# A gated hybrid attention block in float32: the up projection as three matmuls of 256 columns into one half bank, without the copy and addition of two parts

## The chip, the cores and the metric

The kernel runs on one core of a Trainium2 chip. The metric is the device time of one execution in microseconds, as the median of the runs shown. The core's engines work side by side on queues of their own: TensorE multiplies matrices (PE in the profile, and PEld for its loading of weights), VectorE (DVE) and ScalarE (ACT) work on rows of numbers, GpSimd is POOL, and SyncE (SP) issues most transfers from memory.

## The reference, cut to what matters

The block has 256 tokens of width 2048. It mixes three kinds of attention through gates and an output projection, and then runs a feed-forward part of width 5632, all in float32. The change lies in the feed-forward part alone, in the product with `w_up`:

```
h2 = rms_norm(x, g_ffn[l])
u = causal_depthwise_conv(h2 @ w_up[l], conv_w[l], conv_b[l])
u_gate, u_val = jnp.split(u, 2, axis=-1)
x = x + (jax.nn.silu(u_gate) * u_val) @ w_down[l]
```

`h2 @ w_up` is a product of 256 x 2048 by 2048 x 11264. The convolution runs along the tokens, over three of them.

## The kernel before

A float32 product is made here of three products of float32r, the form that TensorE takes at a higher rate. Each operand is split into two parts: `hi`, the value rounded to float32r, and `lo`, the rest. A product is then hi x hi + hi x lo + lo x hi, and lo x lo is dropped. Activations are kept as tiles whose 512 columns are the 256 columns of the hi part followed by the 256 of the lo part (`xT`, `oT`, `mT`, `hT`, `aT`).

Weights come in through `piece`: a transfer on SP's queue brings 128 x 1024 numbers into `raw`, ScalarE rounds them into `hi` (L136), and VectorE subtracts to get `lo` (L137). There are four buffers of each kind. Most stages take the result of `piece` into `passes` (L147 to L149): there the activation is the stationary operand (128 x 128), the weights stream past it with up to 512 columns, and three matmuls in a row add into the same output.

The up projection is turned the other way. There the weights are stationary, 128 of their columns at a time, and the activation `hT` streams past, so that the result has features on partitions and the 256 tokens along its columns, as the convolution wants it. The columns of `w_up` are taken in 22 stripes of 512: for `f0` in steps of 4 over 44 feature tiles, and for `s` = 0 (gate) and 1 (value). A stripe has four feature tiles, each with a bank of PSUM (128 x 512 float32) of its own, from a pool of eight banks. Over 16 tiles `k + j` of the contraction, and for each of the four, two matmuls are issued (L739 and L740): the first takes the `hi` weights past all 512 columns of `hT`, so that hi x hi lands in the left half of the bank and hi x lo in the right half; the second takes the `lo` weights past the left 256 columns of `hT` and adds lo x hi to the left half. That is 44 x 2 x 16 = 1408 pairs.

`conv` then ends a feature tile. ScalarE copies the right half out of PSUM into `cr` (L710), VectorE adds the left half (L712) and multiplies by the row norm `rbc` (L713) into the padded tile `u`; the three taps follow (L716 to L718), then the SiLU (L720) or the product of gate and value and its split into `aT` (L724, L169, L170). `later` puts such work into a queue, and `tick`, which is called after each piece, lets up to two of these pieces of work go on, so that they stand in the engines' queues behind the weights' splitting. After the up projection the down projection (L797 to L799, in `three`) reads `aT`.

Of the kernel before, what the change touches and what calls it, by code (L numbers as in the profile page):

```python
# [9 lines left out]
F32 = mybir.dt.float32  # L10
F32R = mybir.dt.float32r
AF = mybir.ActivationFunctionType
ALU = mybir.AluOpType
AX = mybir.AxisListType

P = 128
S = 256
# [24 lines left out]
def hybrid_block(  # L42
# [25 lines left out]
    nc = tc.nc  # L68
# [12 lines left out]
    def bank(name):  # L81
        return pp.tile([P, 512], F32, tag="bank", name=name)
# [14 lines left out]
    def later(gen):  # L97
        waiting.append(gen)

    def tick():  # L100
        while waiting and len(active) < WINDOW:
            active.append([waiting.popleft(), 0])
        for a in list(active):
            if a[1] > 0:
                a[1] -= 1
                continue
            try:
                a[1] = next(a[0]) or 0
            except StopIteration:
                active.remove(a)  # L110
# [19 lines left out]
    def piece(src, a, n, name):  # L130
        raw = wp.tile([P, PIECE], F32, tag="raw", name=f"raw_{name}")
        hi = wp.tile([P, PIECE], F32R, tag="hi", bufs=SBUFS, name=f"hi_{name}")
        lo = wp.tile([P, PIECE], F32R, tag="lo", bufs=SBUFS, name=f"lo_{name}")
        m = a * n
        nc.sync.dma_start(raw[:, :m].rearrange("p (a n) -> p a n", a=a), src)
        pin(nc.scalar.copy(hi[:, :m], raw[:, :m]))  # L136
        pin(nc.vector.tensor_tensor(lo[:, :m], raw[:, :m], hi[:, :m].bitcast(F32), ALU.subtract))  # L137
        return (
            hi[:, :m].rearrange("p (a n) -> p a n", a=a),
            lo[:, :m].rearrange("p (a n) -> p a n", a=a),  # L140
        )
# [9 lines left out]
    def product(x_of, w, nk, n0, n, name):  # L151

        ps = [bank(f"{name}_{t}") for t in range(NT)]
        wv = w.rearrange("(k p) n -> p k n", p=P)
        for k in range(0, nk, 2):
            a = min(2, nk - k)
            wh, wl = piece(wv[:, k : k + a, n0 : n0 + n], a, n, f"{name}_{k}")
            order = [(j, t) for j in range(a) for t in range(NT)]
            if k + a == nk:
                order.sort(key=lambda jt: jt[1])  # L160
            for j, t in order:
                passes(ps[t][:, :n], x_of(k + j), t, wh[:, j], wl[:, j], k + j == 0, k + j == nk - 1)
            tick()
        return ps

    def split_to(dst, src, g=None):

        if g is None:
            nc.scalar.copy(dst[:, :S], src)  # L169
            nc.vector.tensor_tensor(dst[:, S:], src, dst[:, :S].bitcast(F32), ALU.subtract)  # L170
        else:
            pin(nc.scalar.activation(dst[:, :S], src, AF.Copy, scale=g))
            pin(
                nc.vector.scalar_tensor_tensor(
                    dst[:, S:], src, g, dst[:, :S].bitcast(F32), ALU.mult, ALU.subtract
                )
            )
# [265 lines left out]
    ps = proj(C_MQ, MEM_W, "mq")  # L443
# [33 lines left out]
    for c in range(3):  # L477
        ps = proj(c * 512, 512, f"f{c}")
# [7 lines left out]
    ps = proj(1536, 512, "f3")  # L486
# [3 lines left out]
    ps = proj(2048, 262, "f4")  # L490
# [68 lines left out]
    for c in range(3):  # L559
        ps = proj(C_SB + c * 512, 512, f"s{c}")  # L560
# [4 lines left out]
    ps = proj(C_SB + 1536, 512, "s3")  # L565
# [3 lines left out]
    ps = proj(C_SB + 2048, 256, "s4")  # L569
# [61 lines left out]
    for n in range(4):  # L631
        n0 = n * 512
        gate = []
        for b in range(3):
            bg = gp.tile([P, 512], F32, tag="bg", name=f"bg_{n}_{b}")
            nc.sync.dma_start(bg, b_gate[0, b, n0 : n0 + 512].partition_broadcast(P))
            ps = proj(C_GATE + b * D + n0, 512, f"g{n}_{b}")
# [11 lines left out]
        for i, (w, k0, nk, b) in enumerate(branches):  # L649
            ps = product(lambda k: oT[:, k0 + k], w[0], nk, n0, 512, f"b{n}_{b}")  # L650
# [10 lines left out]
    hT = xt_pool.tile([P, KT, 2 * S], F32R, tag="xt", name="hT")  # L661
    rb = sm.tile([P, 512], F32, tag="junk", bufs=2, name="rb")[:, :S].rearrange("p (t s) -> p t s", t=NT)
    rbc = cst.tile([P, S], F32, name="rbc")
# [17 lines left out]
    for n in range(4):  # L681
        c = slice(n * 512, (n + 1) * 512)
        ps = product(lambda k: mT[k // 2][:, k % 2], w_out[0], KT, n * 512, 512, f"o{n}")
# [9 lines left out]
    cp = uv.enter_context(tc.tile_pool(name="cp", bufs=2))  # L693
# [3 lines left out]
    def padded():  # L697
        for i in range(2):
            u = cp.tile([P, S + 2], F32, bufs=1, name=f"u_{i}")
            nc.vector.memset(u[:, 0:2], 0.0)  # L700
            pads.append(u)
# [3 lines left out]
    def conv(ps, f, s):  # L705
        if not pads:
            padded()
        ct = s * FT + f
        cr = cp.tile([P, S], F32, tag="cr", bufs=2, name=f"cr_{f}_{s}")
        nc.scalar.copy(cr, ps[:, S:])  # L710
        u = pads[f % 2]
        nc.vector.tensor_tensor(cr, cr, ps[:, :S], ALU.add)  # L712
        nc.vector.tensor_tensor(u[:, 2:], cr, rbc, ALU.mult)  # L713
        y = cp.tile([P, S], F32, tag="y", bufs=6, name=f"y_{f}_{s}")
        tap = lambda j: taps[:, j, ct : ct + 1]
        nc.scalar.activation(y, u[:, 2:], AF.Identity, scale=tap(2), bias=tap(3))  # L716
        nc.vector.scalar_tensor_tensor(y, u[:, 1 : S + 1], tap(1), y, ALU.mult, ALU.add)
        nc.vector.scalar_tensor_tensor(y, u[:, 0:S], tap(0), y, ALU.mult, ALU.add)  # L718
        if s == 0:
            nc.scalar.activation(y, y, AF.Silu)  # L720
            ys[f] = y
        else:
            g = ys.pop(f)
            nc.vector.tensor_tensor(g, g, y, ALU.mult)  # L724
            split_to(aT[:, f, :], g)
        return
        yield

    for f0 in range(0, FT, 4):
        for s in range(2):  # L730
            ps = [bank(f"u{f0 + i}_{s}") for i in range(4)]
            c0 = s * D_FF + f0 * P
            for k in range(0, KT, 2):
                hi, lo = piece(upv[:, k : k + 2, c0 : c0 + 512], 2, 512, f"u{f0}_{s}_{k}")
                for j in range(2):
                    first, last = k + j == 0, k + j == KT - 1
                    for i in range(4):
                        c = slice(i * P, (i + 1) * P)
                        nc.tensor.matmul(ps[i], lhsT=hi[:, j, c], rhs=hT[:, k + j, :], start=first, stop=False)  # L739
                        nc.tensor.matmul(  # L740
                            ps[i][:, :S], lhsT=lo[:, j, c], rhs=hT[:, k + j, :S], start=False, stop=last
                        )
                tick()
            for i in range(4):
                later(conv(ps[i], f0 + i, s))
# [121 lines left out]
    for nb, plan in enumerate(plans):  # L867
# [3 lines left out]
        ns, s, e = plan.count("s"), 0, plan.count("s")  # L871
# [13 lines left out]
        for t in range(NT):  # L885
            for n in range(2):
                o = sm.tile([P, 512], F32, tag="junk", bufs=2, name=f"o_{nb}_{t}_{n}")
                parts_ = 2 if (nb, t, n) == (1, 1, 1) else 1
                for i in range(parts_):
                    w = 512 // parts_  # L890
# [35 lines left out]
```

## Time and profile before

| what | value |
|---|---|
| median of the runs (2) | 1497.88 us (1497.55 to 1498.22) |
| span of the profiled execution, first to last instruction | 1494.4 us |
| time of that span against the median | 3.5 us less |
| PE busy, share of the span | 99% |
| PE weight load busy | 84% |
| VectorE busy | 68% |
| ScalarE busy | 53% |
| granted TensorE clock | 1.000 |
| first matmul of the up projection to the first of the down projection | 766.02 to 1255.33 us |

The busy time of PE is a sum over matmuls that overlap, since the end of each is modelled. So the rate of TensorE is read here from the distance between the starts of matmuls that follow each other in the timeline, and not from the durations. A wait shows as idle time in square brackets in the timeline, with the engine that ended it.

### The profile page before, as it was taken

The page shows a single profiled execution, that of the slowest core. Times are in us where ns is not written, and L with a number is a line of the kernel's source. Part 1 is how long each engine was busy: PE and PEld are TensorE (multiplying, and loading weights), DVE is VectorE, ACT ScalarE, POOL GpSimd, SP SyncE. Part 2 cuts the span into 40 slices and gives each one's busy share as a digit, 9 for nine tenths or more (in the row PEclk, how much of TensorE's full clock was granted, in tenths as well). Part 3 has the DMA queues.
Part 4 walks back from the last instruction along what each step waited for, and adds up shares of the span by engine and source line. Part 5 has one row for each costly group of instructions (what it writes and reads, how often), then busy time and mean ns, then how long its engine had stood idle before and what let it go on. Part 6 is the DMA issues. An engine that isn't in the chain of part 4 may idle for free.

```text
span 1494.4 us, 19871 instructions
## 1 busy us (share of the span) xinstructions
PE 1483.2 (99%) x7429; PEld 1255.9 (84%) x7429; DVE 1014.0 (68%) x1465; ACT 794.0 (53%) x1108; POOL 16.1 (1%) x46
## 2 busy tenths in 40 slices
PE   8999999999999999999999999999999999999998
PEld 6888888888888888888888888888888888888777
DVE  5767566555655646555557778777778778987885
ACT  6755454358544444444456556556556656553552
POOL 0000000001000000000000000000000000000000
PEclk9999999999999999999999999999999999999999
DMA  8665475365666666655555665655656565556554
GB/s 291 193 211 158 126 220 167 119 211 164 188 194 210 185 210 203 185 190 190 184 182 183 198 191 184 196 190 184 198 187 191 186 196 183 199 188 228 185 202 140
DMA packets 138543, 283.62 MB, mean 190 GB/s; under 512 B 9275, under 2 KB 18127, under 8 KB 138447
## 3 DMA queue, kind: packets, MB, share of 16 engines
q1 hardware_dynamic: 137118, 280.26, 59.0%
q10 hardware_dynamic: 1328, 2.11, 0.4%
q8 instruction: 58, 0.95, 0.2%
q14 instruction: 39, 0.31, 0.1%
HBM read 280.23 MB, written 2.10 MB: 189 GB/s over the span
## 4 chain that ended last, share of the span: by engine, by line
PE 95%; DMA 2%; ACT 1%; DVE 1%; issue 0%; POOL 0%; SPq 0%; DVEq 0%; POOLq 0%; ACTq 0%
PE u L739 21%; PE u L740 11%; PE g L147 5%; PE g L148 5%; PE g L149 5%; PE x L797 4%; PE x L798 4%; PE x L799 4%; PE s L147 2%; PE s L149 2%; PE f L147 2%; PE f L149 2%; PE s L148 2%; PE f L148 2%; PE o L147 2%; PE o L149 2%
## 5 line engine op out<-in xcount | busy, mean ns | idle before, releaser
L739 PE MATMUL u<-hT,hi_u 128*128 128x512 f32 x1408 | 488.5, 392 | 0.0
L740 PE MATMUL u<-hT,lo_u 128*128 128x256 f32 x1408 | 395.1, 281 | 0.0
L739 PEld LDWEIGHTS u<-hT,hi_u 128*128 128x128 f32 x1408 | 263.3, 187 | 57.3
L137 DVE TENSOR_TENSOR lo_u<-raw_u,hi_u 128x1024 fp32r<-128x1024 f32 x176 | 215.4, 1224 | 116.0 <-ACT hi_u L136 115.9
L740 PEld LDWEIGHTS u<-hT,lo_u 128*128 128x128 f32 x1408 | 266.8, 189 | 0.0
L136 ACT CAST hi_u<-raw_u 128x1024 fp32r<-128x1024 f32 x176 | 184.7, 1050 | 138.4 <-PE u L739 106.5
L137 DVE TENSOR_TENSOR lo_g<-raw_g,hi_g 128x1024 fp32r<-128x1024 f32 x96 | 117.7, 1229 | 101.3 <-ACT hi_g L136 98.8
L136 ACT CAST hi_g<-raw_g 128x1024 fp32r<-128x1024 f32 x96 | 100.7, 1051 | 121.8 <-PE g L148 97.4
L147 PE MATMUL g<-hi_g,xT 128*128 128x512 f32 x384 | 151.1, 393 | 0.0
L149 PE MATMUL g<-lo_g,xT 128*128 128x512 f32 x384 | 149.8, 390 | 0.0
L148 PE MATMUL g<-hi_g,xT 128*128 128x512 f32 x384 | 149.7, 390 | 0.0
L792 ACT CAST hi_d<-raw_d 128x1024 fp32r<-128x1024 f32 (+1 forms) x88 | 86.7, 993 | 74.6 <-PE x L798 38.7
L793 DVE TENSOR_TENSOR lo_d<-raw_d,hi_d 128x1024 fp32r<-128x1024 f32 (+1 forms) x88 | 99.8, 1148 | 16.2 <-ACT hi_d L792 16.2
L797 PE MATMUL x<-hi_d,aT 128*128 128x512 f32 x268 | 104.4, 390 | 0.0
L799 PE MATMUL x<-lo_d,aT 128*128 128x512 f32 x268 | 104.4, 390 | 0.0
L798 PE MATMUL x<-hi_d,aT 128*128 128x512 f32 x268 | 104.4, 390 | 0.0
L149 PEld LDWEIGHTS g<-lo_g,xT 128*128 128x128 f32 x384 | 72.1, 188 | 15.2
L148 PEld LDWEIGHTS g<-hi_g,xT 128*128 128x128 f32 x384 | 72.2, 188 | 14.5
L147 PEld LDWEIGHTS g<-hi_g,xT 128*128 128x128 f32 x384 | 72.2, 188 | 14.6
L137 DVE TENSOR_TENSOR lo_s<-raw_s,hi_s 128x1024 fp32r<-128x1024 f32 (+1 forms) x40 | 44.7, 1118 | 37.2 <-ACT hi_s L136 37.2
L137 DVE TENSOR_TENSOR lo_f<-raw_f,hi_f 128x1024 fp32r<-128x1024 f32 (+1 forms) x40 | 44.7, 1120 | 34.5 <-ACT hi_f L136 33.0
L136 ACT CAST hi_f<-raw_f 128x1024 fp32r<-128x1024 f32 (+1 forms) x40 | 38.5, 966 | 52.5 <-PE f L148 47.6
(318 smaller groups left out, 2554.3 us busy)
## 6 DMA issues: line engine op xcount, KB each, us to landing
raw_u<-in_w_up_dram SPq DMA_DIRECT2D x176, 512.0 KB, 4.0
raw_g<-in_w_in_dram SPq DMA_DIRECT2D x96, 512.0 KB, 3.6
raw_d<-in_w_down_dram SPq DMA_DIRECT2D x88, 512.0 KB, 4.7
raw_f<-in_w_in_dram SPq DMA_DIRECT2D x32, 512.0 KB, 3.5
raw_s<-in_w_in_dram SPq DMA_DIRECT2D x32, 512.0 KB, 3.4
raw_o<-in_w_out_dram SPq DMA_DIRECT2D x32, 512.0 KB, 4.7
raw_kv<-in_w_mem_kv_dram SPq DMA_DIRECT2D x15, 512.0 KB, 5.4
raw_b<-in_w_br_fox_dram SPq DMA_DIRECT2D x12, 512.0 KB, 4.0
```

What stands on the lines that cost most here:

```text
L136: pin(nc.scalar.copy(hi[:, :m], raw[:, :m]))
L137: pin(nc.vector.tensor_tensor(lo[:, :m], raw[:, :m], hi[:, :m].bitcast(F32), ALU.subtract))
L147: nc.tensor.matmul(o, lhsT=xh, rhs=wh, start=first, stop=False)
L148: nc.tensor.matmul(o, lhsT=xl, rhs=wh, start=False, stop=False)
L149: nc.tensor.matmul(o, lhsT=xh, rhs=wl, start=False, stop=last)
L739: nc.tensor.matmul(ps[i], lhsT=hi[:, j, c], rhs=hT[:, k + j, :], start=first, stop=False)
L740: nc.tensor.matmul(ps[i][:, :S], lhsT=lo[:, j, c], rhs=hT[:, k + j, :S], start=False, stop=last)
L792: nc.scalar.copy(hi[:, :n], src)
L793: nc.vector.tensor_tensor(lo[:, :n], src, hi[:, :n].bitcast(F32), ALU.subtract)
L797: nc.tensor.matmul(o, lhsT=ah, rhs=w[0], start=first, stop=False)
L798: nc.tensor.matmul(o, lhsT=al, rhs=w[0], start=False, stop=False)
L799: nc.tensor.matmul(o, lhsT=ah, rhs=w[1], start=False, stop=last)
```

## The change

The pair of matmuls becomes three, each with 256 streamed columns: hi weights by the hi half of `hT`, hi weights by the lo half, lo weights by the hi half. All three add into the same 256 columns, half of a bank, so a bank holds two feature tiles and a stripe takes two banks. Only the first matmul into a bank carries the start flag. The sum of the parts is thereby complete in PSUM, and `conv` loses the copy on ScalarE and the addition on VectorE: its multiplication by `rbc` reads PSUM directly.

```diff
         ct = s * FT + f
-        cr = cp.tile([P, S], F32, tag="cr", bufs=2, name=f"cr_{f}_{s}")
-        nc.scalar.copy(cr, ps[:, S:])
         u = pads[f % 2]
-        nc.vector.tensor_tensor(cr, cr, ps[:, :S], ALU.add)
-        nc.vector.tensor_tensor(u[:, 2:], cr, rbc, ALU.mult)
+        nc.vector.tensor_tensor(u[:, 2:], ps, rbc, ALU.mult)
...
     for f0 in range(0, FT, 4):
         for s in range(2):
-            ps = [bank(f"u{f0 + i}_{s}") for i in range(4)]
+            ps = [b[:, i * S : (i + 1) * S] for b in (bank(f"u{f0}_{s}"), bank(f"u{f0 + 2}_{s}")) for i in range(2)]
             c0 = s * D_FF + f0 * P
             for k in range(0, KT, 2):
                 hi, lo = piece(upv[:, k : k + 2, c0 : c0 + 512], 2, 512, f"u{f0}_{s}_{k}")
@@
                     for i in range(4):
                         c = slice(i * P, (i + 1) * P)
-                        nc.tensor.matmul(ps[i], lhsT=hi[:, j, c], rhs=hT[:, k + j, :], start=first, stop=False)
-                        nc.tensor.matmul(
-                            ps[i][:, :S], lhsT=lo[:, j, c], rhs=hT[:, k + j, :S], start=False, stop=last
-                        )
+                        for l, (w, o) in enumerate(((hi, 0), (hi, S), (lo, 0))):
+                            nc.tensor.matmul(
+                                ps[i], lhsT=w[:, j, c], rhs=hT[:, k + j, o : o + S],
+                                start=first and l == 0 and i % 2 == 0, stop=last and l == 2, skip_group_check=True,
+                            )
```

TensorE's queue at the start of the up projection, before: the four banks of the stripe are `u_0_6213` to `u_0_6216`, and `hi_u`, `lo_u` are the parts of the first piece of weights.

```order
L739 MATMUL u_0_6213<-hT,hi_u_0_0_6218 128x512
L740 MATMUL u_0_6213<-hT,lo_u_0_0_6219 128x256
L739 MATMUL u_0_6214<-hT,hi_u_0_0_6218 128x512
L740 MATMUL u_0_6214<-hT,lo_u_0_0_6219 128x256
L739 MATMUL u_0_6215<-hT,hi_u_0_0_6218 128x512
L740 MATMUL u_0_6215<-hT,lo_u_0_0_6219 128x256
L739 MATMUL u_0_6216<-hT,hi_u_0_0_6218 128x512
L740 MATMUL u_0_6216<-hT,lo_u_0_0_6219 128x256
```

The same place in the changed kernel; `x2` stands for two matmuls that follow each other with the same operands' names.

```order
L737 MATMUL u_0_6213<-hT,hi_u_0_0_6216 128x256 x2
L737 MATMUL u_0_6213<-hT,lo_u_0_0_6217 128x256
L737 MATMUL u_0_6213<-hT,hi_u_0_0_6216 128x256 x2
L737 MATMUL u_0_6213<-hT,lo_u_0_0_6217 128x256
L737 MATMUL u_0_6214<-hT,hi_u_0_0_6216 128x256 x2
L737 MATMUL u_0_6214<-hT,lo_u_0_0_6217 128x256
L737 MATMUL u_0_6214<-hT,hi_u_0_0_6216 128x256 x2
L737 MATMUL u_0_6214<-hT,lo_u_0_0_6217 128x256
```

Each 512-column matmul has become two of 256, in the same place of the queue, and two feature tiles now share a bank. The order of pieces, of transfers and of the other stages on TensorE is the same as before.

## The prediction

> **What bounds the kernel now.** I read the page first: which engine is on the chain that ended last, and with which lines.
>
> ```profile
> span 1494.4 us, 19871 instructions
> PE 1483.2 (99%) x7429; PEld 1255.9 (84%) x7429; DVE 1014.0 (68%) x1465; ACT 794.0 (53%) x1108; POOL 16.1 (1%) x46
> PE 95%; DMA 2%; ACT 1%; DVE 1%; issue 0%; POOL 0%; SPq 0%; DVEq 0%; POOLq 0%; ACTq 0%
> L739 PE MATMUL u<-hT,hi_u 128*128 128x512 f32 x1408 | 488.5, 392 | 0.0
> L740 PE MATMUL u<-hT,lo_u 128*128 128x256 f32 x1408 | 395.1, 281 | 0.0
> ```
>
> TensorE holds 95% of the chain, and its two groups of the up projection have no idle time ahead of them. The counts of PE and PEld are equal, 7429 each: every matmul brings a weight load of its own. The 392 and 281 ns are durations with modelled ends that overlap, so they are no prices. The next view is the stage by itself, in the windows, from its first matmul to the first of the down projection (the columns are each engine's busy time with its count, the granted clock, and the share and rate of transfers):
>
> ```profile
> 766.02:1255.33 489.31, 489.31 (x2828) 431.90 (x2826) 366.58 (x607) 289.74 (x443) 0.00 (x0) 1.00 0.60 189
> ```
>
> PE is busy for all of 489.31 us at a clock of 1.00, DVE for 366.58 and ACT for 289.74. The third view is the waits of the other engines inside this stretch and the groups of the vector work:
>
> ```profile
> ACT hi_u L136 <- PE u L739: 106.5, 93, 2.0
> L713 DVE TENSOR_TENSOR u<-cr,rbc 128x256 f32<-128x256 f32 x88 | 34.2, 420 | 0.0
> L712 DVE TENSOR_TENSOR cr<-cr,u 128x256 f32<-128x256 f32 x88 | 34.1, 418 | 0.0
> L710 ACT COPY cr<-u 128x256 f32<-128x256 f32 x88 | 29.4, 365 | 16.9 <-PE u L740 16.9
> ```
>
> ScalarE waits 106.5 us in all for TensorE to hand back a buffer of weights. So the helpers run ahead as far as their buffers let them, and TensorE sets the pace. What a change does to the time of this stage is what it does to the distance between the starts of TensorE's matmuls.
>
> **What the pair costs now.** Here is the timeline of PE in the middle of the stage, eight pairs from the first row to the last:
>
> ```profile
> 899.65 0.39 PE L739 MATMUL u<-hT,hi_u 128*128 128x512 f32 x1
> 899.88 0.28 PE L740 MATMUL u<-hT,lo_u 128*128 128x256 f32 x1
> 900.00 0.39 PE L739 MATMUL u<-hT,hi_u 128*128 128x512 f32 x1
> 900.23 0.28 PE L740 MATMUL u<-hT,lo_u 128*128 128x256 f32 x1
> ...
> 902.42 0.39 PE L739 MATMUL u<-hT,hi_u 128*128 128x512 f32 x1
> ```
>
> (902.42 - 899.65) / 8 = 346.3 ns for a pair. Over the whole stage it is a little more: 489.31 us less the eight transposes of `hT` that stand in it,
>
> ```profile
> 771.83 0.87 PE hT L184 x8
> ```
>
> at most 0.87 us in the chain of waits, leaves 488.4 us, and divided by 1408 that is 346.9 ns. I take 347 ns.
>
> **What the three will cost.** The trace of before holds just such a stream: the last column block of the stick-breaking projection is only 256 wide, and there `passes` issues three matmuls of 256 columns in a row into the same 256 columns, each with other 128 x 128 weights, in float32r, at the same clock. The rows of the groups, and the first and last starts:
>
> ```profile
> L149 PE MATMUL s<-lo_s,xT 128*128 128x256 f32 x32 | 9.1, 283 | 0.0
> L148 PE MATMUL s<-hi_s,xT 128*128 128x256 f32 x32 | 9.1, 283 | 0.0
> L147 PE MATMUL s<-hi_s,xT 128*128 128x256 f32 x32 | 9.1, 283 | 0.0
> ```
>
> ```profile
> 295.72 0.39 PE L148 MATMUL s<-hi_s,xT 128*128 128x512 f32 x1
> ...
> 297.99 0.39 PE L149 MATMUL s<-lo_s,xT 128*128 128x512 f32 x1
> 298.21 0.28 PE L147 MATMUL s<-hi_s,xT 128*128 128x256 f32 x1
> ...
> 309.73 0.40 PE L147 MATMUL g<-hi_g,xT 128*128 128x512 f32 x1
> ```
>
> From 298.21 to 309.73 us there are 3 x 32 = 96 starts: 11.52 / 96 = 120.0 ns for one matmul of 256 columns. The ten matmuls of 512 columns ahead of them, 295.72 to 297.99, take 227 ns each. One of 512 and one of 256 make 227 + 120 = 347 ns, which is the pair of the up projection: the two prices explain the stage as it is. Two of 256 make 240, which is 13 ns above one of 512. In numbers of this trace, a matmul costs a part that grows with its columns, (227 - 120) / 256 = 0.418 ns each, and a fixed part of 120 - 256 x 0.418 = 13 ns. Splitting the 512 columns in two keeps the first and pays the second once more. I use 3 x 120.0 = 360 ns against 347.
>
> A second block agrees: one that is 262 columns wide, from 184.24 to the first of the next block at 195.93, again 96 matmuls.
>
> ```profile
> 184.24 0.28 PE L147 MATMUL f<-hi_f,xT 128*128 128x262 f32 x1
> ...
> 195.93 0.40 PE L147 MATMUL s<-hi_s,xT 128*128 128x512 f32 x1
> ```
>
> 11.69 / 96 = 121.8 ns, and 262 x 0.418 + 13 = 122.5.
>
> The first two of the three have the same weights. I count a full load for each, since where this kernel does the same it loads each time: the nine matmuls at the start, all by `idle`, have nine loads.
>
> ```profile
> L91 PEld LDWEIGHTS <-idle x9: 104/151/151, 1.2 to 5.0; 128*128 128x128 bf16 x9
> L91 PE MATMUL spare<-idle x9: 327/527/528, 1.2 to 5.3; 128*128 128x384 bf16 x9
> ```
>
> **The sum.** 13 ns x 1408 = 18.3 us more on TensorE, all of it on the path, for there is no wait of TensorE in this stage that could take it up. From the steady 346.3 ns it would be 13.7 x 1408 = 19.3 us, from the 262-wide rate 3 x 121.8 - 347 = 18.4 ns, or 25.9 us. The other end is nought, if two halves cost just what the whole did; below that it does not go, since the same 768 columns stream past.
>
> The vector work that goes, 88 copies of 365 ns and 88 additions of 418 ns, some 29 us of ACT and 34 us of DVE, lies wholly beside TensorE: ACT's and DVE's totals in the stage are 200 and 123 us below its length. I count nothing for it. The remaining multiplication (420 ns) now reads PSUM where it read SBUF; L712 does read PSUM, with 418 ns, so nothing there either. If the cover were gone, what is removed would be worth at most the longer of the two, 34 us.
>
> One place remains where less vector work could let TensorE go earlier: behind the stage, in the down projection, TensorE waits for VectorE twice (waits of PE, then two links of the chain).
>
> ```profile
> PE y L799 <- DVE lo_t L793: 2.2, 2, 1.4
> ```
>
> ```profile
> 1387.46 4.04 DMA raw_d<-in_w_down_dram
> 1392.13 1.23 DVE lo_t L793
> ```
>
> The chain has the first of these at 1392 us, over 130 us after the stage ended, and a transfer stands ahead of it, so I leave the 2.2 us where they are; between -2.2 and 0. The transfers move the same bytes in 507.6 us instead of 489.3, so memory cannot become the bound.
>
> The profiled span goes from 1494.4 to 1494.4 + 18.3 = 1512.7 us. The median of the runs stands 3.5 us above the span, which I keep: 1516.2 us, 1.2% slower. A measurement of this kernel can tell about 2% from no change, so this counts as within that bound.
>
> **A rule beside the row.** The Trainium skill, "TensorE: Matmul & The Clock Gate", section "Back-to-back issue gap", gives the isolated spacing of matmuls at full clock as N / 2.4 + 2.5 ns, so 109 ns for 256 columns and 216 for 512. By that the split would cost 2.5 ns x 1408 = 3.5 us, for a time of 1501.4. This trace has the slope (0.418 against 1 / 2.4 = 0.417 ns) but a fixed part of 13 ns where each matmul brings its load.
>
> **Rivals.** A: the split is nearly free, and the kernel is not measurably slower. Place: the second hi matmul, whose weights are in the array already. What speaks for it: inside the pair, the starts show the 512 at 0.23 us and the 256 at (2.77 - 8 x 0.23) / 8 = 0.116, and three of 116.3 ns make 349, which is 2 ns over 347; 1408 x 2 = 2.8 us, time 1500.7 us. If the fixed part belongs to a change of weights, the second hi matmul doesn't pay it, and the time stays at 1497.9. It decides if three matmuls take under 350 ns. Against it: 96 in a row at 120.0, and 227 + 120 matching the pair, which says that the 0.23 and 0.116 only shift a few ns between neighbours.
>
> B: the weight loads become the bound. A load shows 187 ns,
>
> ```profile
> L739 PEld LDWEIGHTS u<-hT,hi_u 128*128 128x128 f32 x1408 | 263.3, 187 | 57.3
> ```
>
> and three of them one after the other are 561 ns, 214 above the pair, or 301 us more: 1799 us. It decides from the point where a load cannot start before the last one's end. Against it stand the 256-wide rows: there a matmul starts every 120 ns, each with its load, so loads do overlap. A smaller form remains possible, a load of weights equal to those in use that has to wait: with one serial load of 187 ns among the three it is 120 + 120 + 187 = 427, so 80 x 1408 = 113 us, 1611 us.
>
> C: emptying the half banks holds TensorE up. A bank is now shared by two feature tiles and comes free when both have been multiplied out. The last stripe's convolutions read PSUM until 1261 us, six after its last matmul (first ACT's timeline, then DVE's).
>
> ```profile
> 1254.49 0.72 ACT L710 COPY cr<-u 128x256 f32<-128x256 f32 x2 [0.80 <-PE u L740]
> ```
>
> ```profile
> 1261.23 0.42 DVE L712 TENSOR_TENSOR cr<-cr,u 128x256 f32<-128x256 f32 x1
> ```
>
> If each of 22 stripes waited these 6 us, it would cost 132 us: 1648 us. Against it: a stripe takes 22 us and two of eight banks, so three stripes fit in before a bank is wanted again.
>
> **How the numbers follow.** Forecast 0.80, A 0.11, B 0.05, C 0.03; 0.01 is left for a gain over 2%, for which I see no mechanism. Forecast and A lie within 2% (1467.9 to 1527.8), so same 0.91; B and C give slower 0.08; faster 0.01. The range takes the forecast with its upper bound of 25.9 us mostly in (1522), and reaches down past the middle towards A (1504).
>
> **What would show it.** Right: the stage between the first `u` matmul and the first `x` matmul lasts 507 to 509 us, three starts take 360 ns, PEld fills the stage (three loads of 187 ns overlap in 360) with 1408 x 3 loads, PE still has no idle ahead of `u`; DVE and ACT in the stage are lower by about 34 and 29 us; the stages before and after keep their lengths within 1 us. Wrong: fewer loads than matmuls, or three starts in 350 ns (A), in 400 ns or more (B), or idle time of PE at the start of stripes with DVE as releaser (C).

## The result and the profile after

The changed kernel takes 1515.46 us (median of 2 runs, 1514.46 to 1516.46) against 1497.88: a ratio of 1.0113, 95% interval 1.0097 to 1.0129. A second comparison on one chip gave 1.0120 (1.0106 to 1.0134). The forecast was 1516.2 us.

The page of the changed kernel, with the lines that answer to those shown of before:

```profile
span 1514.8 us, 22547 instructions
PE 1503.0 (99%) x8837; PEld 1332.6 (88%) x8837; DVE 987.3 (65%) x1377; ACT 767.8 (51%) x1020; POOL 16.2 (1%) x46
PE 93%; DMA 3%; DVE 2%; ACT 1%; issue 1%; POOL 0%; DVEq 0%; SPq 0%; POOLq 0%; ACTq 0%
L737 PE MATMUL u<-hT,hi_u 128*128 128x256 f32 x2816 | 507.1, 283 | 0.0
L737 PEld LDWEIGHTS u<-hT,hi_u 128*128 128x128 f32 x2816 | 439.3, 192 | 0.1
L737 PE MATMUL u<-hT,lo_u 128*128 128x256 f32 x1408 | 398.5, 283 | 0.0
L737 PEld LDWEIGHTS u<-hT,lo_u 128*128 128x128 f32 x1408 | 270.3, 192 | 0.0
```

PE and PEld have 1408 instructions more each, so the second hi matmul loads its weights again. TensorE still has no idle ahead of `u`. The up projection by itself, from its first matmul to the first of the down projection, in the windows (busy time by engine, then clock, share and rate of transfers):

```profile
764.23:1272.18 507.95, 507.95 (x4236) 507.94 (x4234) 341.61 (x523) 263.17 (x358) 0.00 (x0) 1.00 0.61 183
```

It lasts 507.95 us where it lasted 489.31: 18.64 us more. The timeline shows the step of three:

```profile
899.22 0.40 PE L737 MATMUL u<-hT,hi_u 128*128 128x256 f32 x2
899.46 0.28 PE L737 MATMUL u<-hT,lo_u 128*128 128x256 f32 x1
...
902.82 0.40 PE L737 MATMUL u<-hT,hi_u 128*128 128x256 f32 x2
```

(902.82 - 899.22) / 10 = 360 ns for three, 120.0 each. VectorE and ScalarE are busy 25 and 27 us less in the stage than before, and TensorE's pace took no notice. What ScalarE saved went into waiting for TensorE, 180.8 us where it was 106.5:

```profile
ACT hi_u L136 <- PE u L737: 180.8, 125, 2.1
```

The whole span grew by 20.4 us. What the stage does not account for lies outside it: 1.8 us less ahead of it and 3.5 us more behind it. With nothing changed, a second profile moves these stretches by up to 1.5 and 6.1 us (below).

### The profile page after: what moved, and what is told of

It reads as the page before. It is cut to its first block, busy times and chain, and to the rows that moved or that the text cites. A ratio compares the mean times of both kernels' runs of the same rounds, so it can differ in the third digit from the quotient of the medians.

```text
span 1514.8 us, 22547 instructions
## 1 busy us (share of the span) xinstructions
PE 1503.0 (99%) x8837; PEld 1332.6 (88%) x8837; DVE 987.3 (65%) x1377; ACT 767.8 (51%) x1020; POOL 16.2 (1%) x46
## 4 chain that ended last, share of the span: by engine, by line
PE 93%; DMA 3%; DVE 2%; ACT 1%; issue 1%; POOL 0%; DVEq 0%; SPq 0%; POOLq 0%; ACTq 0%
PE u L737 33%; PE g L147 5%; PE g L148 5%; PE g L149 5%; PE x L795 3%; PE x L796 3%; PE x L797 3%; PE s L147 2%; PE s L149 2%; PE f L147 2%; PE f L148 2%; PE s L148 2%; PE f L149 2%; PE o L147 2%; PE o L149 2%; PE o L148 2%
## 5 line engine op out<-in xcount | busy, mean ns | idle before, releaser
L737 PE MATMUL u<-hT,hi_u 128*128 128x256 f32 x2816 | 507.1, 283 | 0.0
L737 PEld LDWEIGHTS u<-hT,hi_u 128*128 128x128 f32 x2816 | 439.3, 192 | 0.1
L136 ACT CAST hi_u<-raw_u 128x1024 fp32r<-128x1024 f32 x176 | 184.0, 1046 | 192.3 <-PE u L737 180.8
L737 PEld LDWEIGHTS u<-hT,lo_u 128*128 128x128 f32 x1408 | 270.3, 192 | 0.0
L713 ACT ACTIVATE y<-u,taps 128x256 f32<-128x256 f32 x88 | 49.4, 597 | 42.0 <-DVE u L710 41.4
```

What stands on the lines that cost most here:

```text
L737: nc.tensor.matmul(ps[i], lhsT=w[:, j, c], rhs=hT[:, k + j, o : o + S], start=first and l == 0 and i % 2 == 0, stop=last and l == 2, skip_ ...
```

## Experiments: which part of the change carries the cost

Three kernels were run beside the change on one chip. The first keeps its matmuls and orders them so that no two neighbours share weights or output.

```diff
-                    for i in range(4):
-                        for l, (w, o) in enumerate(((hi, 0), (hi, S), (lo, 0))):
+                    for l, (w, o) in enumerate(((hi, 0), (hi, S), (lo, 0))):
+                        for i in range(4):
```

> The changed kernel, with its three parts in the outer loop and the four feature tiles in the inner one: neighbours on TensorE now share neither weights nor output. Theory 1 (each matmul pays 13 ns beside its columns, whatever its neighbour): the same as the change, 360 ns for three, up stage 508 us, about 1.1% over the kernel before. Rival (neighbours with the same weights, or three additions in a row into the same columns, have a price or a discount of their own): the stage differs from the change's 507.95 us by more than 3 us, either way.

Ratio 1.0115 (1.0099 to 1.0130), stage 763.67 to 1271.62 us, 507.95 us. In this stage neighbours play no part. A second matmul with the same weights is no cheaper than one with others, and three additions in a row into the same columns are no dearer.

The second and the third each do half of the change.

```diff
-        cr = cp.tile([P, S], F32, tag="cr", bufs=2, name=f"cr_{f}_{s}")
-        nc.scalar.copy(cr, ps[:, S:])
-        nc.vector.tensor_tensor(cr, cr, ps[:, :S], ALU.add)
-        nc.vector.tensor_tensor(u[:, 2:], cr, rbc, ALU.mult)
+        nc.vector.tensor_tensor(u[:, 2:], ps[:, :S], rbc, ALU.mult)
```

> The kernel before, its pair of matmuls untouched, but without the copy and the addition of the two parts: the multiplication reads the left half alone, so hi x lo is left out of the result. Theory 1 (vector work lies beside TensorE): stage 489 us, ratio to the kernel before 1.000 within 0.2%. Rival (the vector work that went is worth something, and part of the split's cost was given back): up to 34 us of DVE, at least 3 us less, ratio below 0.998.

Ratio 0.9996 (0.9988 to 1.0005). Windows of the stage:

```profile
764.29:1253.61 489.32, 489.32 (x2828) 432.13 (x2827) 339.78 (x523) 263.77 (x358) 0.00 (x0) 1.00 0.64 189
```

VectorE is down to 339.78 us, ScalarE to 263.77, and the stage has its 489.3 us. The copy and the addition were worth nothing that these runs can show.

```diff
-   nc.tensor.matmul(ps[i], lhsT=hi[:, j, c], rhs=hT[:, k + j, :], start=first, stop=False)
-   nc.tensor.matmul(ps[i][:, :S], lhsT=lo[:, j, c], rhs=hT[:, k + j, :S], start=False, stop=last)
+   for l, (w, o, d) in enumerate(((hi, 0, 0), (hi, S, S), (lo, 0, 0))):
+       nc.tensor.matmul(ps[i][:, d : d + S], lhsT=w[:, j, c], rhs=hT[:, k + j, o : o + S], ...)
```

> The kernel before with its banks, copy and addition, and only the 512-column matmul issued as two of 256, into the left and the right half. Theory 1: all of the change's cost is here, stage 508 us, ratio 1.012, the same as the change. Rival (sharing of half banks, or the multiplication from PSUM, carries part of the cost): stage under 503 us, ratio under 1.009.

Ratio 1.0106 (1.0092 to 1.0120). The windows:

```profile
763.23:1271.17 507.94, 507.94 (x4235) 507.94 (x4234) 368.31 (x607) 291.31 (x443) 0.00 (x0) 1.00 0.63 183
```

With the old banks and all of the old vector work, the stage has the change's 507.94 us. So the split alone makes the cost, and sharing banks adds nothing. The change itself, repeated beside them:

> The change once more, on the chip of the three kernels beside it. Stage 508 us, ratio 1.011 to 1.013. The profiled run before had 3.5 us more behind the stage (5.2 us of TensorE's waits for lo_t in the down projection against 2.2) and 1.8 us less ahead of it, where the two programs are alike. If that is scatter, these two stretches move again by some us; if it belongs to the change, the stretch behind the stage is again 242 to 243 us against 239.

Ratio 1.0120 (1.0106 to 1.0134), stage 765.44 to 1273.39, again 507.95 us. Its span of 1517.6 us leaves 244.2 us behind the stage. The kernel before was profiled once more too:

> The kernel before, for another profile: its stage 489.3 us. Behind the stage it had 239.07 us in its first profile, where five kernels with the same down projection have 241.8 to 244.2. If that was scatter, this profile has 241 us or more; if the change adds to it, 239 again.

```profile
span 1499.0 us, 19871 instructions
764.50:1253.81 489.31, 489.31 (x2828) 432.02 (x2827) 366.56 (x607) 289.76 (x443) 0.00 (x0) 1.00 0.65 189
PE y L799 <- DVE lo_t L793: 7.6, 6, 1.8
```

It has 245.2 us behind the stage, 7.6 us of them TensorE's waits for `lo_t`. So the stretch behind varies from 239 to 245 us in one and the same program, and the stretch ahead from 763 to 766 us over these kernels. The first profile of before fell on the short side behind and the long side ahead. Nothing ties these differences to the change (behind the stage, before had 239.1 and 245.2 us, the change 242.6 and 244.2), while the stage repeats to 0.01 us.

## Experiments: does the price belong to the place

All 1152 matmuls of the gate products that stream 512 columns are split instead; there the activation is loaded and the weights stream.

```diff
+        if halves:
+            for l, (a, w) in enumerate(((xh, wh), (xl, wh), (xh, wl))):
+                for n in (0, S):
+                    nc.tensor.matmul(o[:, n : n + S], lhsT=a, rhs=w[:, n : n + S], ...)
+            return
```

> The kernel before, its up projection untouched; instead all 3 x 384 = 1152 matmuls of 512 columns in the gate products are issued as two of 256 into the halves of the same bank, with the same weights for both. Theory 1: 1152 x 13.2 ns = 15.2 us more, ratio 1.010. Rival (the price belongs to the up projection's arrangement, with w_up as the stationary operand): no more than 3 us, ratio under 1.002.

Ratio 1.0079 (1.0064 to 1.0094); the interval just misses the expected 1.010. The up projection keeps its 489.31 us (its window is the first row). TensorE's timeline in the split products shows 120.0 ns, (341.37 - 339.93) / 12:

```profile
777.68:1266.99 489.31, 489.31 (x2827) 432.11 (x2826) 366.49 (x607) 289.82 (x443) 0.00 (x0) 1.00 0.65 190
```

```profile
339.93 0.64 PE L150 MATMUL g<-hi_g,xT 128*128 128x256 f32 x4
340.41 0.40 PE L150 MATMUL g<-lo_g,xT 128*128 128x256 f32 x2
...
341.37 0.64 PE L150 MATMUL g<-hi_g,xT 128*128 128x256 f32 x4
```

The last three quarters of the gate stage (864 splits, with the branch products that stand between them) took 411.63 to 686.93 us here and 409.65 to 673.74 in the second profile of before: 11.2 us more, 13.0 ns for each split. The first quarter, with attention's matmuls in between, grew by only 2.5 us (from 308.19 to 409.65 in the second profile of before, 307.63 to 411.63 here), 8.8 ns for each of its 288 splits; why it lost less is not shown. In the three quarters without them the price carries over.

## Experiments: what the 13 ns are

With half of the weight columns loaded, the streamed columns as before:

```diff
+   m = P if first else P // 2
-   c = slice(i * P, (i + 1) * P)
+   c = slice(i * P, i * P + m)
-   ps[i], lhsT=w[:, j, c], ...
+   ps[i][:m], lhsT=w[:, j, c], ...
```

> The change with only 64 of 128 weight columns in each matmul of the up projection, but for the first of 16 contraction tiles, so half of each feature tile is left without most of its sum. Each matmul still streams 256 columns. Theory 1 (a fixed 13 ns for each matmul, whatever it loads): three still take 360 ns, stage 508 us, ratio 1.012. Rival (the 120 ns are the time in which 128 weight columns load, a floor under narrow matmuls): loads halve, the stream decides, at least 256 x 0.418 = 107 ns a matmul, so 13 x 3 x 1320 = 51 us less: stage about 457 us, ratio 0.977. In between: part of the 13 ns grows with the columns loaded.

The stage fell between the two, to 482.37 us, ratio 0.9933 (0.9917 to 0.9950). Its window, and the timeline of PE:

```profile
763.85:1246.22 482.37, 482.37 (x4235) 482.37 (x4234) 339.69 (x523) 263.83 (x357) 0.00 (x0) 1.00 0.64 192
```

```profile
905.15 0.28 PE L738 MATMUL u<-hT,lo_u 128*64 128x256 f32 x1
...
908.55 0.28 PE L738 MATMUL u<-hT,lo_u 128*64 128x256 f32 x1
```

Ten steps of three in 3.40 us: 340 ns, 113.3 each. So at 256 streamed columns half of the 13 ns goes with half of the load, and theory 1 fails where fewer columns are loaded. That suggested a price for each loaded column, and two more loads were tried: the same half in the kernel before's pair, and a quarter in the change.

> The kernel before with its pair of matmuls, but only 64 of 128 weight columns for all but the first of 16 contraction tiles (half of each feature tile is left without most of its sum). Where three matmuls of 256 went from 120.0 to 113.6 ns each by this, two theories are left. Theory 2 (each matmul pays some 0.104 ns for each weight column that it loads, also under 512 streamed columns): the pair loses 2 x 6.6 ns, 333.6 ns, stage 489.3 - 1320 x 0.0133 = 471.8 us. Rival (the load of 128 columns is a floor that touches only matmuls as narrow as 256; a 512 hides it): only the 256 gains, pair 340.5 ns, stage 480.9 us.

The stage lasted 480.47 us, close to the rival's 480.9. From 904.90 to 908.30 the timeline again has ten steps of 340 ns. If the 256 takes 113.3 of them, as in the run above, 226.7 are left for the 512, which is what it takes with a full load, so only the 256 got shorter.

```profile
765.29:1245.76 480.47, 480.47 (x2828) 353.20 (x2827) 364.94 (x607) 289.01 (x443) 0.00 (x0) 1.00 0.65 193
```

```profile
904.90 0.27 PE L741 MATMUL u<-hT,lo_u 128*64 128x256 f32 x1
905.01 0.39 PE L740 MATMUL u<-hT,hi_u 128*64 128x512 f32 x1
...
908.30 0.27 PE L741 MATMUL u<-hT,lo_u 128*64 128x256 f32 x1
```

With half loads, pair and three cost the same, 340 ns: there the split is free.

> The change with only 32 of 128 weight columns, but for the first contraction tile (three quarters of each feature tile are left without most of their sum). Theory 2 (0.104 ns for each loaded column): a matmul of 256 takes 106.7 + 3.3 = 110 ns, three 330, stage 508 - 1320 x 0.030 = 468.3 us. Rival (a part of some 7 ns stays with each matmul whatever it loads): as with 64 columns, 482 us.

A quarter of the load brought nothing more: the stage took 491.52 us, and no stripe reached 330 ns. But for the first stripe, those of the gate (`s` = 0) run at 340 ns for three, as with half the load, and those of the value (`s` = 1) at 353. Here are the windows of the stage and of two stripes that follow each other:

```profile
764.23:1255.75 491.52, 491.52 (x4236) 459.92 (x4235) 339.99 (x523) 263.55 (x358) 0.00 (x0) 1.00 0.63 189
810.68:832.55 21.87, 21.87 (x194) 20.85 (x193) 16.71 (x29) 11.82 (x16) 0.00 (x0) 1.00 0.62 189
832.55:855.19 22.64, 22.64 (x195) 20.86 (x194) 14.41 (x22) 11.87 (x17) 0.00 (x0) 1.00 0.64 189
```

Theory 2 fell with both runs. The rival's 482 us was missed too, by 9.5 us, and no run shows why the two kinds of stripes differ. The next run loads half of the rows instead of half of the columns:

> The change with only 64 of 128 rows of weights and of hT, but for the first contraction tile, so that half of the sum is left out; all 128 weight columns are loaded. Theory 2 (the price goes by weight columns): as the change, stage 508 us. Rival (it goes by the amount of weights loaded, rows or columns): 113.6 ns a matmul, stage 482 us.

Three take 360 ns in a steady stretch (900.07, 900.43, 900.79 us for the lo matmul): halving the rows saves nothing there, where halving the columns did. The stage as a whole was longer than with all rows, 516.31 us. The rows at a change from 64 to 128 rows show where:

```profile
883.88 0.28 PE L738 MATMUL u<-hT,lo_u 64*128 64x256 f32 x1
884.09 0.50 PE L738 MATMUL u<-hT,hi_u 128*128 128x256 f32 x2
884.43 0.28 PE L738 MATMUL u<-hT,lo_u 128*128 128x256 f32 x1
```

Between the starts 0.21 us stand where 0.12 would, and 0.34 where 0.24 would: 0.19 us more. There are 44 such changes in the stage, 22 in each direction if the one at its end is counted, which makes the 8.4 us that it is longer.

Then the widths. One of 384 and one of 128 columns instead of 512:

> The kernel before (its banks, copy and addition), with the 512-column matmul issued as one of 384 and one of 128 columns. Theory 1: 384 x 0.418 + 13 = 173.5 and 128 x 0.418 + 13 = 66.5, together 240 as with two of 256: stage 508 us. Rival, the load as a floor of 120 ns: 173.5 + 120 + 120 = 413.5 ns for three, stage 583 us, 75 us over the change. A third way, that float32r is streamed at a lower rate below some width: the 128 columns take longer than 120 ns and the stage is over 590 us.

The stage took 573.67 us, ratio 1.0545 (1.0524 to 1.0566), near the rival's 583 and far from 508: some 407 ns for three. The timeline of matmuls and loads (PEld rows are weight loads):

```profile
900.33 0.40 PE L740 MATMUL u<-hT,hi_u 128*128 128x384 f32 x2
900.50 0.19 PEld L740 LDWEIGHTS u<-hT,lo_u 128*128 128x128 f32 x1
900.56 0.33 PE L740 MATMUL u<-hT,lo_u 128*128 128x256 f32 x1
900.61 0.31 PEld L740 LDWEIGHTS u<-hT,hi_u 128*128 128x128 f32 x2
900.73 0.41 PE L740 MATMUL u<-hT,hi_u 128*128 128x384 f32 x2
```

The load for lo starts at 900.50, the next at 900.61, and its 384 at 900.73: two loads in 0.23 us, 0.115 each, although the row of the single load shows a duration of 0.19. Read so, a load of 128 columns needs some 0.115 us of its own, and a matmul of 128 streamed columns is too short to hide one. A floor of that sort was now a third theory also for the 256, whose 120.0 ns lie just above. The last run was to separate them, by a width that takes longer than such a load.

```diff
+   for l, (w, o) in enumerate(((hi, 0), (hi, 128), (lo, 0))):
+       nc.tensor.matmul(ps[i][:, o : o + 384], lhsT=w[:, j, c], rhs=hT[:, k + j, o : o + 384], ...)
```

> The kernel before (its banks, copy and addition), with three matmuls of 384 columns in place of the pair: hi weights by columns 0 to 383 and by 128 to 511 of hT, lo weights by 0 to 383, so that some products are counted twice or needn't be there. All load 128 weight columns, and the stream of 384 columns is longer than any load. Theory 1, as the prediction had it (0.418 ns a column and a fixed 13 ns for each matmul): 173.5 ns each, 520.5 for three, stage 733.5 us. Theory 3, drawn from the half loads (0.443 ns a column and nothing fixed, but never under 120 ns with a load of 128 weight columns): 170 ns each, 510 for three, stage 718.8 us.

```profile
764.05:1497.37 733.32, 733.32 (x4236) 733.25 (x4235) 376.74 (x608) 292.82 (x444) 0.00 (x0) 1.00 0.44 127
```

```profile
899.89 0.51 PE L740 MATMUL u<-hT,hi_u 128*128 128x384 f32 x2
...
902.49 0.51 PE L740 MATMUL u<-hT,hi_u 128*128 128x384 f32 x2
```

Five steps in 2.60 us: 520 ns for three, 173.3 each, and the stage took 733.32 us (764.05 to 1497.37) against the expected 733.5 and 718.8. Theory 1 has the figure for full loads, and theory 3 as it was written fails. With full loads the three widths measured are 120.0, 173.3 and 226.7 ns for 256, 384 and 512 columns (the last is the 346.7 ns of a pair in the steady part of a stripe, less 120.0): 0.417 ns a column and 13.3 ns a matmul.

A floor under the 256 is not out by this, though. Theory 3 drew a straight line from 113.3 ns (256 columns) to 226.7 (512), and no run shows that 384 columns lie on it. Moreover 113.3, 120.0, 173.3 and 226.7 ns are 17, 18, 26 and 34 times 6.67 ns, while 170 is 25.5 times. If TensorE can start matmuls only in such steps, theory 3's 170 becomes 173.3 as well. That is a pattern in these figures, and no run was made to test it.

So what the 13.3 ns are stays open. All the steps measured with full, half and quarter loads at widths of 256 to 512 are met, but for the 353 ns stripes, by 0.417 ns a column plus the larger of two parts: 0.104 ns for each loaded column (13.3 for 128, 6.7 for 64) and 0.026 ns for each streamed one (13.3 for 512, 6.7 for 256). By it the load sets the price of the 256, and half of its 13.3 ns is there only because 128 columns are loaded. That is a description made after these runs, and not tested by another.

## Why the prediction was right, point by point

- **The bound.** Right, and shown by the two halves of the change: TensorE alone sets the stage; with the pair kept, 27 us of VectorE and 26 of ScalarE less moved it by 0.01 us, and the split alone made all of the difference.
- **The price of three.** 360 ns were taken from a stretch of 96 matmuls of the same kind that the kernel already held. Measured: 360. The pair was put at 347, and the sum of 18.3 us came out as 18.64.
- **Fixed part and slope.** They were drawn from two widths. A third width bears them out, and so does the split at another place. They hold for loads of 128 columns only. The prediction called the 13 ns a fixed part of each matmul, and that name is too strong: with 64 loaded columns half of it is gone at 256 streamed columns. The forecast needed only the price of the 256 with a full load, which it had measured.
- **Same weights.** Right: each of the two hi matmuls loads, 4224 loads in the stage, and the run with its neighbours apart shows no discount. Rival A is out. Its 116 ns for the 256 inside the pair did not become the price of three, as the prediction said.
- **The rule beside the row.** By the Trainium skill, "TensorE: Matmul & The Clock Gate", section "Back-to-back issue gap", the time would have been 1501.4 us; 1515.46 was measured. The slope agrees with the runs, the 2.5 ns of overhead do not: they are 13.3 ns here, where each matmul has its own load of 128 columns.
- **Rival B.** Its 427 and 561 ns for three are out: 360 were measured. But the rows against it were read loosely. Loads with rows of 187 ns do overlap, and still they followed each other no faster than 115 ns or so in the run with 384 and 128 columns. The change's 120 ns lie just above that, and with half loads they fall to 113.3, so a small part of the price may be the load's after all.
- **Rival C.** Out: no idle ahead of `u`, and with half banks or whole ones the stage is the same to 0.01 us.
- **Vector work removed.** Expected 34 and 29 us less busy time, measured 25 and 27. Rows on these engines overlap with their neighbours' (88 additions of 418 ns would be 36.8 us, and the busy time of the group is 34.1), so less goes with a group than its row shows. The multiplication kept its 420 ns when it read PSUM:

```profile
L710 DVE TENSOR_TENSOR u<-u,rbc 128x256 f32<-128x256 f32 x88 | 35.0, 420 | 0.0
```

- **The stages around.** "Within 1 us" was wrong for a single pair of profiles: -1.8 and +3.5 us. A second profile of before moved by 6 us in the same stretch with nothing changed, so the tolerance was too tight. That the forecast of 1516.2 us met the median within 0.7 us is in part luck, since these stretches alone scatter by more.

## What to carry to other kernels

Where TensorE is busy throughout, count its instructions as well as the streamed columns: in this kernel, splitting one matmul of 512 into two of 256 costs 13 ns each time with a full load of weights, and work taken off engines that already wait for TensorE paid nothing back. Look for a stretch in the kernel's own trace that already runs the new form, and price the change by starts there, not by durations. With 128 streamed columns the loading of weights seems to set the pace, and that cost several times more: the split into 384 and 128 took the pair from 347 to some 407 ns.

## What had not been expected of the hardware

- With 64 loaded weight columns, 512 + 256 and 3 x 256 cost the same, 340 ns; with 128 they differ, 347 against 360. With 32 columns there was nothing more to gain, and in about half of the stripes it was 353.
- Loads whose rows show 187 to 192 ns can start some 115 ns apart; matmuls with half the rows take as long as those with all of them (360 ns for three).
- A change between 64 and 128 rows costs some 0.19 us each time.
- The four prices measured, 113.3, 120.0, 173.3 and 226.7 ns, are whole multiples of 6.67 ns; whether that is a rule is not tested.
